# Score products of a pair's two heads, issued alternately into two PSUM banks

## The chip, the cores and the metric

The kernel runs on one core of one Trainium2 chip. The metric is the device time of one execution in microseconds (us); lower is better. The engines are named as in the profile: PE is the matrix engine (PEld its weight loads), DVE the vector engine, ACT the scalar engine, POOL GpSimd, SP the engine that issues the transfers.

## The reference

One decoder layer on 512 tokens of 1024 features, in fp32: a half-step of a gated feed-forward network, a token mixer, a second such half-step, and a gated embedding. The mixer is attention in a sliding window, with sinks, beside a causal convolution. Cut to what the change touches:

```python
q = partial_rope(rmsnorm(zq.reshape(B, S, 16, 64), q_norm), cos, sin)
k = partial_rope(rmsnorm(zk.reshape(B, S, 2, 64), k_norm), cos, sin)
# in sliding_window_attention: blocks of 128 queries, each with its own and the previous 128 keys
s = einsum('bnqhgd,bnkhd->bnhgqk', qb, kb) * scale
s = where(valid, s, -1e30)
m = maximum(max(s, axis=-1), sink)
pr = exp(s - m)
denom = sum(pr, axis=-1) + exp(sink - m)
o = einsum('bnhgqk,bnkhd->bnqhgd', pr / denom, vb)
...
u = causal_depthwise_conv(ca * sigmoid(cb), dw_w, dw_b)        # 31 taps
merged = sigmoid(ga) * (o @ attn_proj) + sigmoid(gb) * (silu(layernorm(u)) @ conv_proj)
x = x + merged @ w_out
```

There are 16 query heads of 64 features and 2 key heads, so 8 query heads share a key head.

## The kernel before

**Products.** Every fp32 operand is split into two parts, hi and lo. A product is three matmuls into one PSUM bank (`mm3`, lines 112 to 115): lo by hi (line 113), hi by hi (114), hi by lo (115). The hi part is made by ACT (line 88), the lo part by DVE (line 89; by POOL for the gates' weights). Parts are named by their endings _h and _l, those of weights whi and wlo.

**PSUM.** The eight banks are two pools of four: `pf` for projections (gates, convolution inputs, queries), `ps` for all else, the scores among it.

**Attention.** The heads stand in eight pairs: pair j holds query head j, whose features and key lie on the lower 64 partitions, and head j + 8, on the upper 64. A group g (0 or 1) is four pairs, a block t (0 to 3) 128 queries, so there are eight blocks (g, t). `scores` (lines 409 to 442) transposes a block's queries (qTp, split to qT), then makes eight score products of 64 partitions by 128 queries and 256 keys (128 keys at t = 0), which is 24 matmuls. Two products share a bank. In before the loop runs over the half hh, the half's two banks jj, and a bank's two pairs jl: all of a half before the other. After each product one DVE operation (line 438) masks and scales it to SBUF (s) and takes its row maximum (m). Four banks hold two rounds of what the trace calls sc. `softmax` (from line 444) takes the exponentials on ACT (454), the denominators on DVE (455, 456), and scales on POOL and ACT; `values` transposes the probabilities (pT, line 472), splits them (p_h, p_l) and multiplies them by the values into one bank (o), which ACT copies out (oF, line 484).

**Beside it** run the convolution's 31 taps for eight tiles of channels: on DVE (line 325) for five of them; for tiles 0, 2 and 4 ACT multiplies (ct, line 322) and POOL adds (323). Further the projections of the convolution's inputs (ca, cb), the queries (q_b), the gates (ga, gb), and attention's output (ap). sga and sgb are gates read out of PSUM by DVE.

**The order.** The string ORDER lists the mixer's parts in the order in which the program hands them over, and the convolution has a lower priority. The framework's scheduler then puts each engine's instructions into an order by its own simulated times, so that parts interleave, and an edit in one place moves instructions of all engines.

Of the kernel before, what the change touches and what calls it, by code (L numbers as in the profile page):

```python
# [15 lines left out]
P = 128  # L16
S = 512
NT = S // P
# [6 lines left out]
HD = 64  # L25
# [6 lines left out]
EPS = 1e-6  # L32
PIECE = 1024


# The order in which the mixer's parts are issued: K keys and values, Q a half of the queries;
# A scores, E softmax, V values of one block; a, b the convolution's input and its gate;
# g, h the gates' projections; p attention's projection; L the convolution's norm.
ORDER = """
# [7 lines left out]
def hybrid_layer(ctx: ExitStack, tc: tile.TileContext, a: dict, out: bass.AP):  # L47
    nc = tc.nc
# [35 lines left out]

# [1 line left out]
    def split_into(hi, lo, src, scale=None, eng=nc.vector):  # L86
# [14 lines left out]
    def piece(src, eng=nc.vector):  # L101
        """A weight piece [P, n] from DRAM as its two parts."""
        n = src.shape[1]
        raw = wraw.tile([P, PIECE], F32, tag="raw", name="raw")
        hi = wspl.tile([P, PIECE], F32R, tag="hi", name="whi")
        lo = wspl.tile([P, PIECE], F32R, tag="lo", name="wlo")
        nc.sync.dma_start(raw[:, 0:n], src)
        split_into(hi[:, 0:n], lo[:, 0:n], raw[:, 0:n], eng=eng)
        return hi, lo

    def mm3(ps, w, x, start, stop):
        """ps += w.T @ x of operands in two parts."""
        nc.tensor.matmul(ps, w[1], x[0], start=start, stop=False)  # L113
        nc.tensor.matmul(ps, w[0], x[0], start=False, stop=False)  # L114
        nc.tensor.matmul(ps, w[0], x[1], start=False, stop=stop)  # L115
# [3 lines left out]

# [1 line left out]
    def rsqrt(name, v, n):  # L121
        """1/sqrt(v) of a small positive tile by Newton's iteration."""
        y = small.tile([P, n], F32, tag=f"y{n}", name=f"{name}_y", bufs=2 if n > 8 else 4)
# [15 lines left out]
    def colsum(name, acc):  # L139
        """Sums over the partitions of [P, S], tokens on partitions: [P, NT] in PSUM."""  # L140
        ps = ps_tile(f"{name}_cs")
        for t in range(NT):
            nc.tensor.matmul(
                ps[:, t : t + 1], acc[:, t * P : (t + 1) * P], ones[:, 0:1], start=True, stop=True
            )
        return ps[:, 0:NT]
# [7 lines left out]
    def spread(name, r):  # L154
        """[P, NT], tokens on partitions, to [P, S] with tokens on the free axis, on each partition."""
        dg = tmp.tile([P, NT, P], F32, tag="t", name=f"{name}_dg")
# [27 lines left out]

# [1 line left out]
    g_all = const.tile([P, 8, KD], F32, name="g_all")  # L186
# [23 lines left out]
    def consts():  # L210
# [19 lines left out]

        # the gains of q's and k's unrotated parts are both k's
        qcs, kcs = table("qcs", gq), table("kcs", gk)
# [3 lines left out]
    def ffn(tag, wgu, wdown, h, ss, first, after):  # L236
        """x += 0.5 * swiglu; `after` takes each new tile of x."""
        rb = None
# [45 lines left out]

# [1 line left out]
    def proj(tag, w_piece, h, nk=KD, off=0, bank=None):  # L286
        """One [P, S] tile of h @ w, features on partitions."""
        ps = (bank or pf_tile)(tag)
# [20 lines left out]

    # depthwise causal convolution; some channels' taps are ScalarE's and GpSimd's  # L310
    def conv(c):
# [14 lines left out]

    # q, k, v with tokens on partitions
    def heads_rsqrt(tag, zs, n, scale):
        """scale / sqrt(mean of squares + EPS) of each head of each block of tokens."""
        v = small.tile([P, NT * n], F32, tag=f"hv{n}", name=f"{tag}_v", bufs=2)  # L330
# [9 lines left out]
    def rope(tag, z3, n, tab, t):  # L340
        """Gain and rotation of the rotated part of each head, in place."""
        w = tmp.tile([P, n, 16], F32, tag="rope", name=f"{tag}_w", bufs=2)
# [7 lines left out]
    def token_major(tag, pieces, kper, n):  # L350
        """h2.T @ w for each block of tokens: NT tiles in PSUM, several to a bank when they are small."""
        per = S // n
# [14 lines left out]
    kT = [rtile(f"kT{i}") for i in range(2)]  # L367
    # each part of v as [v0, 0, v1], so that a pair's heads take their own half of a column
    vp = [act.tile([P, 2, 3, HD], F32R, tag="a", name=f"v{t}", bufs=NBIG) for t in range(NT)]
# [25 lines left out]
    def queries(g):  # L395
        """Four pairs of heads (j, j + 8) of the queries, rotated; their norm and the scores' scale are in rq."""
        pss = token_major(f"q{g}_", [a["wq"][4 * g + i] for i in range(4)], 2, S)
# [11 lines left out]
    def scores(g, t):  # L409
        """Masked scores of eight heads (four pairs) of one block of queries, and their maxima."""  # L410
        pt = ps_tile(f"qTp{g}_{t}")
# [14 lines left out]
        mask = masks[:, min(t, 1), 0:nk]  # L426
        for hh in range(2):
            rows = slice(hh * HD, (hh + 1) * HD)
            for jj in range(2):
                ps = ps_tile(f"sc{g}_{t}_{hh}_{jj}").rearrange("p (j k) -> p j k", j=2)  # L430
                i0 = hh * 2 + jj
                for jl in range(2):
                    j = 2 * jj + jl
                    q = [qT[i][rows, j * P : (j + 1) * P] for i in range(2)]
                    kk = [kT[i][rows, k0 : k0 + nk] for i in range(2)]
                    mm3(ps[:, jl, 0:nk], q, kk, True, True)
                    i = 2 * i0 + jl
                    nc.vector.tensor_tensor_reduce(
                        s[i0][:, jl, 0:nk], ps[:, jl, 0:nk], mask, rq[g][t][:, 2 * j + hh : 2 * j + hh + 1],
                        sk[:, i : i + 1], ALU.add, ALU.max, m[:, i : i + 1],  # L440
                    )
# [63 lines left out]
    def attn_proj(o):  # L505
        """Attention's projection under its gate."""
        if o == 0:
# [15 lines left out]
    def conv_norm():  # L523
        """Layer norm over channels, then silu."""
        acc = tmp.tile([P, S], F32, tag="acc", name="ln_acc", bufs=2)
# [48 lines left out]

# [1 line left out]
    h4, ss4, after4 = next_norm("pg", g_gate)  # L576
# [11 lines left out]

# [1 line left out]
    rb4 = None  # L590
# [31 lines left out]
def _layout(inputs):  # L622
    """The inputs as the program reads them, and tables that depend on shapes alone."""
    import numpy as np
# [6 lines left out]
    def kxn(w):  # L631
        """[K, N] -> [N/128 tiles][128 of K, K/128, 128 of N]."""
        kt, nt = w.shape[0] // P, w.shape[1] // P
# [32 lines left out]

    rows = lambda v: np.broadcast_to(v, (P, v.shape[-1]))  # noqa: E731
    gains = np.stack(
# [53 lines left out]
```

## Time and profile before

| | us |
|---|---|
| median of 3 runs | 1309.3 |
| lowest, highest | 1308.62, 1310.32 |
| span of the profiled execution | 1306.9 |
| PE busy in it | 1241.3 |
| DVE busy | 804.9 |
| ACT busy | 496.8 |
| POOL busy | 379.5 |

The span is the time from the first to the last instruction of one profiled execution; the median lies 2.4 us above it. Numbers of the trace are told against the span's start. In a row of the timeline stand the start, the duration, the engine, the line, the operation, out<-in, the shapes and how many instructions the row joins, and in brackets how long the engine had been idle and what it waited for. In a row of waits stand who waited, for whom, the total in us, the times and the longest. In a row of stretches each engine's busy time is followed by its count of instructions in brackets, and at the end stand PE's granted clock (1.00 is full speed), the share of the DMA engines and GB/s.

### The profile page before, as it was taken

To read this page: it belongs to the slowest core of one execution; us is meant where nothing else is said; L and a number is where in the kernel's file an instruction comes from. 1 tells how busy PE (TensorE), PEld (TensorE's weight loads), DVE (VectorE), ACT (ScalarE), POOL (GpSimd) and SP (SyncE) were. 2 spreads that over 40 slices of the span, in tenths; PEclk is the share of its full clock that TensorE was granted. 3 is DMA by queue.
4 is the path that set the end of the run, shared out by engine and by line. 5 is a ranking of instruction groups with operands and counts; after the bars stand their busy time and mean duration, and the time that the engine had idled before them with its cause. 6 is when DMAs were issued, how large, how long until landed. Compare 5 with 4: busy or idle time off the path is not lost.

```text
span 1306.9 us, 14445 instructions
## 1 busy us (share of the span) xinstructions
PE 1241.3 (95%) x5534; PEld 1015.0 (78%) x5534; DVE 804.9 (62%) x1076; ACT 496.8 (38%) x789; POOL 379.5 (29%) x322
## 2 busy tenths in 40 slices
PE   7999999999999878786889999999999999999998
PEld 5888888888888666565767878888888888888886
DVE  7544444434448988999999665575444444444447
ACT  5333333222225457563755454333333333222242
POOL 4000000011116979867687350050000000011140
PEclk9999999999999989898988999999999999999999
DMA  6223222333322212121011123232232223333331
GB/s 210 97 97 97 97 97 97 89 100 94 101 95 71 80 49 65 49 65 49 17 49 65 65 97 113 81 113 83 97 99 98 95 97 98 96 89 105 109 97 65
DMA packets 35206, 115.27 MB, mean 88 GB/s; under 512 B 4416, under 2 KB 5952, under 8 KB 35136
## 3 DMA queue, kind: packets, MB, share of 16 engines
q1 hardware_dynamic: 34992, 114.31, 27.2%
q8 instruction: 43, 0.70, 0.2%
q14 instruction: 27, 0.22, 0.1%
q10 hardware_dynamic: 144, 0.03, 0.0%
HBM read 112.23 MB, written 2.10 MB: 87 GB/s over the span
## 4 chain that ended last, share of the span: by engine, by line
PE 75%; DVE 18%; ACT 3%; POOL 2%; issue 2%; DMA 0%; SPq 0%; DVEq 0%; POOLq 0%
DVE y L325 10%; PE f_d L114 6%; PE f_d L113 6%; PE f_d L115 6%; PE f_g L115 6%; PE f_u L115 6%; PE f_g L114 6%; PE f_g L113 6%; PE f_u L114 6%; PE f_u L113 6%; DVE wlo L89 2%; POOL y L323 1%; ACT s L454 1%; PE cp L113 1%; PE wo L115 1%
## 5 line engine op out<-in xcount | busy, mean ns | idle before, releaser
L88 ACT ACTIVATE whi<-raw 128x1024 fp32r<-128x1024 f32 (+1 forms) x210 | 219.4, 1045 | 566.9 <-PE f_u L115 258.6
L89 DVE TENSOR_TENSOR wlo<-raw,whi 128x1024 fp32r<-128x1024 f32 (+1 forms) x194 | 258.1, 1331 | 240.6 <-ACT whi L88 240.5
L325 DVE SCALAR_TENSOR_TENSOR y<-u,c_dww,y 128x511 f32<-128x511 f32 (+15 forms) x150 | 171.7, 1156 | 1.4
L323 POOL TENSOR_TENSOR y<-y,ct 128x511 f32<-128x511 f32 (+14 forms) x90 | 127.3, 1415 | 35.0 <-ACT ct L322 29.5
L113 PE MATMUL f_d<-f_a_h,wlo 128*128 128x512 f32 x352 | 137.1, 390 | 0.0
L115 PE MATMUL f_d<-f_a_l,whi 128*128 128x512 f32 x352 | 137.1, 389 | 0.0
L114 PE MATMUL f_d<-f_a_h,whi 128*128 128x512 f32 x352 | 137.1, 389 | 0.0
L257 DVE TENSOR_TENSOR f_gs<-f_g,f_n_rb 128x512 f32<-128x512 f32 x44 | 30.4, 691 | 104.7 <-PE f_g L115 95.9
L322 ACT ACTIVATE ct<-u,c_dww 128x511 f32<-128x511 f32 (+14 forms) x90 | 62.4, 707 | 65.7 <-POOL y L323 65.2
L113 PEld LDWEIGHTS f_d<-f_a_h,wlo 128*128 128x128 f32 x352 | 66.1, 188 | 13.8
L115 PEld LDWEIGHTS f_d<-f_a_l,whi 128*128 128x128 f32 x352 | 66.1, 188 | 13.7
L114 PEld LDWEIGHTS f_d<-f_a_h,whi 128*128 128x128 f32 x352 | 66.1, 188 | 13.6
L180 POOL TENSOR_TENSOR pg_ss_acc<-xt 128x512 f32<-128x512 f32 x1 | 1.0, 1040 | 252.9 <-DVE xt L270 252.9
L180 POOL TENSOR_TENSOR mix_ss_acc<-xt 128x512 f32<-128x512 f32 x1 | 1.0, 1039 | 235.2 <-DVE xt L270 235.2
L113 PE MATMUL f_u<-f_h_h,wlo 128*128 128x512 f32 x176 | 69.0, 392 | 0.0
L113 PE MATMUL f_g<-f_h_h,wlo 128*128 128x512 f32 x176 | 68.7, 390 | 0.0
L115 PE MATMUL f_u<-f_h_l,whi 128*128 128x512 f32 x176 | 68.6, 390 | 0.0
L114 PE MATMUL f_g<-f_h_h,whi 128*128 128x512 f32 x176 | 68.6, 390 | 0.0
L114 PE MATMUL f_u<-f_h_h,whi 128*128 128x512 f32 x176 | 68.6, 390 | 0.0
L115 PE MATMUL f_g<-f_h_l,whi 128*128 128x512 f32 x176 | 68.6, 390 | 0.0
L113 PE MATMUL f_u<-h_h,wlo 128*128 128x512 f32 x168 | 65.9, 392 | 0.0
L115 PE MATMUL f_u<-h_l,whi 128*128 128x512 f32 x168 | 65.5, 390 | 0.0
(320 smaller groups left out, 2883.7 us busy)
## 6 DMA issues: line engine op xcount, KB each, us to landing
raw<-in_wgu SPq DMA_DIRECT2D x86, 512.0 KB, 3.5
raw<-in_wd SPq DMA_DIRECT2D x32, 512.0 KB, 3.6
raw<-in_wzc SPq DMA_DIRECT2D x16, 512.0 KB, 3.5
raw<-in_wzg SPq DMA_DIRECT2D x16, 512.0 KB, 3.4
raw<-in_wd SPq DMA_DIRECT2D x16, 384.0 KB, 3.1
raw<-in_wq SPq DMA_DIRECT2D x8, 512.0 KB, 3.4
raw<-in_wap SPq DMA_DIRECT2D x8, 512.0 KB, 3.5
raw<-in_wcp SPq DMA_DIRECT2D x8, 512.0 KB, 3.4
```

Source lines behind the costliest of these rows:

```text
L88: nc.scalar.activation(hi, src, AF.Copy)
L89: eng.tensor_tensor(lo, src, hi.bitcast(F32), op=ALU.subtract)
L113: nc.tensor.matmul(ps, w[1], x[0], start=start, stop=False)
L114: nc.tensor.matmul(ps, w[0], x[0], start=False, stop=False)
L115: nc.tensor.matmul(ps, w[0], x[1], start=False, stop=stop)
L180: nc.gpsimd.tensor_tensor(to, v, v, op=ALU.mult)
L257: nc.vector.tensor_tensor(g, pg, rb, op=ALU.mult)
L322: nc.scalar.activation(t, ud, AF.Copy, scale=wk)
L323: nc.gpsimd.tensor_tensor(yd, yd, t, op=ALU.add)
L325: nc.vector.scalar_tensor_tensor(yd, ud, wk, yd, op0=ALU.mult, op1=ALU.add)
L454: nc.scalar.activation(si, si, AF.Exp, bias=nm[:, i : i + 1], accum_out=den[:, i : i + 1])
```

## The change

`scores` takes two banks at a time, one for each half hh, and issues the three matmuls of the two halves' products alternately; the two DVE readings follow the six matmuls. The diff also takes comments and docstrings out, and all lines below move by ten (the reading is line 448 instead of 438).

```diff
-        for hh in range(2):
-            rows = slice(hh * HD, (hh + 1) * HD)
-            for jj in range(2):
-                ps = ps_tile(f"sc{g}_{t}_{hh}_{jj}").rearrange("p (j k) -> p j k", j=2)
-                i0 = hh * 2 + jj
-                for jl in range(2):
-                    j = 2 * jj + jl
-                    q = [qT[i][rows, j * P : (j + 1) * P] for i in range(2)]
-                    kk = [kT[i][rows, k0 : k0 + nk] for i in range(2)]
-                    mm3(ps[:, jl, 0:nk], q, kk, True, True)
+        for jj in range(2):
+            pss = [
+                ps_tile(f"sc{g}_{t}_{hh}_{jj}").rearrange("p (j k) -> p j k", j=2) for hh in range(2)
+            ]
+            for jl in range(2):
+                j = 2 * jj + jl
+                for n, (a_, b_) in enumerate(((1, 0), (0, 0), (0, 1))):
+                    for hh in range(2):
+                        rows = slice(hh * HD, (hh + 1) * HD)
+                        nc.tensor.matmul(
+                            pss[hh][:, jl, 0:nk],
+                            qT[a_][rows, j * P : (j + 1) * P],
+                            kT[b_][rows, k0 : k0 + nk],
+                            start=n == 0,
+                            stop=n == 2,
+                        )
+                for hh in range(2):
+                    i0 = hh * 2 + jj
                     i = 2 * i0 + jl
                     nc.vector.tensor_tensor_reduce(
-                        s[i0][:, jl, 0:nk], ps[:, jl, 0:nk], mask, rq[g][t][:, 2 * j + hh : 2 * j + hh + 1],
+                        s[i0][:, jl, 0:nk], pss[hh][:, jl, 0:nk], mask, rq[g][t][:, 2 * j + hh : 2 * j + hh + 1],
```

The instructions stay the same in kind and number. Their order changes on PE, DVE, ACT and POOL from the first score product on; SP's stays. Three places follow; the digits behind sc are t, hh and jj and the bank's running number, those behind p and pT are t, hh, the block of keys and the running number.

PE, first round of the block g = 0, t = 0, before and then now:

```order
L113 MATMUL sc_0_0_0_3258<-kT_2548,qT_0_l 128x128
L114 MATMUL sc_0_0_0_3258<-kT_2548,qT_0_h 128x128
L115 MATMUL sc_0_0_0_3258<-kT_2549,qT_0_h 128x128
L113 MATMUL sc_0_0_1_3267<-kT_2548,qT_0_l 128x128
L114 MATMUL sc_0_0_1_3267<-kT_2548,qT_0_h 128x128
L115 MATMUL sc_0_0_1_3267<-kT_2549,qT_0_h 128x128
L113 MATMUL sc_0_1_0_3276<-kT_2548,qT_0_l 128x128
```

Now the same block begins so on PE:

```order
L438 MATMUL sc_0_0_0_3258<-kT_2548,qT_0_l 128x128
L438 MATMUL sc_0_1_0_3259<-kT_2548,qT_0_l 128x128
L438 MATMUL sc_0_0_0_3258<-kT_2548,qT_0_h 128x128
L438 MATMUL sc_0_1_0_3259<-kT_2548,qT_0_h 128x128
L438 MATMUL sc_0_0_0_3258<-kT_2549,qT_0_h 128x128
L438 MATMUL sc_0_1_0_3259<-kT_2549,qT_0_h 128x128
L438 MATMUL sc_0_0_1_3276<-kT_2548,qT_0_l 128x128
```

The halves alternate within the first round, and a bank's third product comes fifth instead of third. In the second round, which begins when DVE has read the banks, the scheduler puts two matmuls of one bank side by side in places:

```order
L438 MATMUL sc_0_0_0_3258<-kT_2548,qT_0_l 128x128
L438 MATMUL sc_0_0_0_3258<-kT_2548,qT_0_h 128x128
L438 MATMUL sc_0_1_0_3259<-kT_2548,qT_0_l 128x128
L438 MATMUL sc_0_1_0_3259<-kT_2548,qT_0_h 128x128
L438 MATMUL sc_0_0_0_3258<-kT_2549,qT_0_h 128x128
L438 MATMUL sc_0_1_0_3259<-kT_2549,qT_0_h 128x128
```

There the pairs of one bank's first two matmuls stand together, and only the last two alternate.

ACT, block g = 1, t = 1 (p_3 are the splits of the probabilities of group 0's last block, es and s the exponentials of this one, ct the products of a tap), before:

```order
L88 ACTIVATE p_3_0_1_h<-pT_3_0_1_4521 128x512
L88 ACTIVATE p_3_1_0_h<-pT_3_1_0_4530 128x512
L88 ACTIVATE p_3_1_1_h<-pT_3_1_1_4539 128x512
L448 ACT_TABLE_LOAD
L448 ACTIVATE es_1_4596<-es_1_4596 128x8
L454 ACTIVATE s_1_0_4469,den_1_4601<-s_1_0_4469,nm_1_4599 128x256 x2
L454 ACTIVATE s_1_1_4470,den_1_4601<-s_1_1_4470,nm_1_4599 128x256 x2
L454 ACTIVATE s_1_2_4471,den_1_4601<-s_1_2_4471,nm_1_4599 128x256 x2
L454 ACTIVATE s_1_3_4472,den_1_4601<-s_1_3_4472,nm_1_4599 128x256 x2
L322 ACTIVATE ct_6_4108<-u_4089,c_dww 128x506
```

The same place on ACT now:

```order
L88 ACTIVATE p_3_0_1_h<-pT_3_0_1_4521 128x512
L322 ACTIVATE ct_6_4108<-u_4089,c_dww 128x506
L88 ACTIVATE p_3_1_0_h<-pT_3_1_0_4530 128x512
L458 ACT_TABLE_LOAD
L458 ACTIVATE es_1_4596<-es_1_4596 128x8
L464 ACTIVATE s_1_0_4469,den_1_4601<-s_1_0_4469,nm_1_4599 128x256 x2
L464 ACTIVATE s_1_1_4470,den_1_4601<-s_1_1_4470,nm_1_4599 128x256 x2
L464 ACTIVATE s_1_2_4471,den_1_4601<-s_1_2_4471,nm_1_4599 128x256 x2
L88 ACTIVATE p_3_1_1_h<-pT_3_1_1_4539 128x512
L464 ACTIVATE s_1_3_4472,den_1_4601<-s_1_3_4472,nm_1_4599 128x256 x2
```

The split p_3_1_1_h moved from ahead of the table load to behind six exponentials, and the tap ct_6 from behind them to ahead of it. On DVE p_3_1_1_l stands in both orders ahead of the convolution input u and the denominators den_1; now one tap more (482 columns) stands ahead of these splits.

DVE, the last block's splits of the probabilities (g = 1, t = 3; y_4838 is the convolution's last tile, and the second number of its shape tells the tap), before:

```order
L89 TENSOR_TENSOR p_3_0_0_l<-pT_3_0_0_5382,p_3_0_0_h 128x512
L325 SCALAR_TENSOR_TENSOR y_4838<-u_4836,c_dww,y_4838 128x488
L89 TENSOR_TENSOR p_3_0_1_l<-pT_3_0_1_5391,p_3_0_1_h 128x512
L325 SCALAR_TENSOR_TENSOR y_4838<-u_4836,c_dww,y_4838 128x487
L89 TENSOR_TENSOR p_3_1_0_l<-pT_3_1_0_5400,p_3_1_0_h 128x512
L325 SCALAR_TENSOR_TENSOR y_4838<-u_4836,c_dww,y_4838 128x486
L325 SCALAR_TENSOR_TENSOR y_4838<-u_4836,c_dww,y_4838 128x485
L325 SCALAR_TENSOR_TENSOR y_4838<-u_4836,c_dww,y_4838 128x484
L325 SCALAR_TENSOR_TENSOR y_4838<-u_4836,c_dww,y_4838 128x483
```

The same place on DVE now:

```order
L325 SCALAR_TENSOR_TENSOR y_4838<-u_4836,c_dww,y_4838 128x487
L89 TENSOR_TENSOR p_3_0_0_l<-pT_3_0_0_5382,p_3_0_0_h 128x512
L89 TENSOR_TENSOR p_3_0_1_l<-pT_3_0_1_5391,p_3_0_1_h 128x512
L325 SCALAR_TENSOR_TENSOR y_4838<-u_4836,c_dww,y_4838 128x486
L325 SCALAR_TENSOR_TENSOR y_4838<-u_4836,c_dww,y_4838 128x485
L325 SCALAR_TENSOR_TENSOR y_4838<-u_4836,c_dww,y_4838 128x484
L89 TENSOR_TENSOR p_3_1_0_l<-pT_3_1_0_5400,p_3_1_0_h 128x512
L325 SCALAR_TENSOR_TENSOR y_4838<-u_4836,c_dww,y_4838 128x483
```

The taps of 486, 485 and 484 columns moved from behind p_3_1_0_l to ahead of it. The split p_2_1_1_l, some ten places earlier, has the taps of 489 and 488 ahead of it that stood behind it, and on PE three products of a gate (ga) moved ahead of the matmul that takes it.

Smaller moves of the same kind: on DVE a tap (503 columns, tile 3) now stands ahead of the first reduction q_v of group 1's query norm, which takes a result of POOL (q_sq); on ACT one tap's product (ct 26 of tile 0) stands ahead of the first table load, and in the block g = 0, t = 1 both p_h of block 0 stand ahead of the exponentials, with one tap's product between them, where one of them stood among them.

## The prediction

> **What bounds the kernel now.** I read the page first: the busy times, the 40 slices and the chain that ended last. Then the busy times of stretches, the waits of PE and of DVE, and at last single rows of the timeline.
>
> ```profile
> span 1306.9 us, 14445 instructions
> PE 1241.3 (95%) x5534; PEld 1015.0 (78%) x5534; DVE 804.9 (62%) x1076; ACT 496.8 (38%) x789; POOL 379.5 (29%) x322
> DVE  7544444434448988999999665575444444444447
> PE 75%; DVE 18%; ACT 3%; POOL 2%; issue 2%; DMA 0%; SPq 0%; DVEq 0%; POOLq 0%
> ```
>
> PE is busy for 95% of the span, which invites the conclusion that any PE time saved is time won. The DVE slices say otherwise for one part: slices 13 to 22 (a slice is 32.7 us) read 8 or 9, and the chain that ended last lies on DVE for 18% of the span. That part is the token mixer, and it holds all the score products. The busy times there, with three smaller stretches and the whole rest of the program:
>
> ```profile
> 440.00:720.00 280.00, 233.60 (x1059) 183.44 (x1058) 265.93 (x416) 160.84 (x355) 220.38 (x190) 0.90 0.16 52
> 610.00:620.00 10.00, 6.49 (x27) 5.59 (x28) 10.00 (x25) 1.54 (x3) 5.04 (x3) 0.50 0.17 53
> 720.00:1300.00 580.00, 578.49 (x2559) 477.10 (x2558) 307.74 (x375) 189.56 (x240) 86.83 (x50) 1.00 0.29 95
> 510.00:520.00 10.00, 10.00 (x55) 8.20 (x54) 8.96 (x15) 5.80 (x9) 9.92 (x12) 1.00 0.33 105
> 550.00:570.00 20.00, 20.00 (x91) 15.56 (x89) 18.86 (x40) 13.87 (x31) 10.53 (x13) 0.91 0.22 67
> ```
>
> The columns after the length are PE, weight loads, DVE, ACT and POOL, then PE's granted clock. From 440 to 720 us DVE is busy for 265.93 of 280 (95%), PE for 233.60 (83%); from 720 on PE is busy for 578.49 of 580. So the mixer goes at DVE's pace, and the rest at PE's. What PE waits for in the mixer, and after it:
>
> ```profile
> PE sc L113 <- DVE m L438: 17.8, 6, 8.2
> PE sc L113 <- DVE qT_l L89: 9.1, 2, 7.5
> PE pT L472 <- DVE m L438: 5.0, 5, 1.8
> PE o L115 <- DVE p_l L89: 4.3, 3, 3.1
> ```
>
> ```profile
> PE ap L113 <- DVE wlo L89: 1.3, 1, 1.3
> PE o L115 <- DVE p_l L89: 0.7, 1, 0.7
> ```
>
> The first four alone are 36.2 us, all for DVE, and the largest is a score product that waits until DVE has read its bank. In the second list (712 us to the end) almost nothing is left: the 1.3 us stand behind DVE's work on the convolution's norm, which itself is released by PE and so moves with it. Hence the **end** is the moment at which DVE releases PE for the last time in the mixer, plus a tail of PE work that the change leaves alone. That moment is this row, a product of the last block's values, 0.72 us late for DVE's split of the probabilities:
>
> ```profile
> 711.68 0.50 PE L115 MATMUL o<-p_l,v 128*128 128x512 f32 x1 [0.72 <-DVE p_l L89]
> 698.26 5.31 DVE L325 SCALAR_TENSOR_TENSOR y<-u,c_dww,y 128x492 f32<-128x492 f32 x3
> 711.55 2.98 DVE L325 SCALAR_TENSOR_TENSOR y<-u,c_dww,y 128x486 f32<-128x486 f32 x4
> ```
>
> The two rows of DVE give the price of a convolution tap, on which much below rests: 5.31 / 3 = 1.77 us while POOL adds beside it, 2.98 / 4 = 0.745 us while POOL doesn't.
>
> **The change part by part. The products themselves.** There are 192 matmuls of 64 partitions, three to a score product; they start this far apart:
>
> ```profile
> 485.77 0.28 PE L114 MATMUL sc<-kT,qT_h 64*128 64x256 f32 x1
> 485.89 0.28 PE L115 MATMUL sc<-kT,qT_h 64*128 64x256 f32 x1
> ...
> 474.01 0.27 PE L113 MATMUL sc<-kT,qT_l 64*128 64x128 f32 x1
> 474.12 0.27 PE L114 MATMUL sc<-kT,qT_h 64*128 64x128 f32 x1
> ```
>
> The step is 0.12 us with 256 columns and 0.11 with 128, so it isn't the moving columns that set it: 192 x 0.115 = 22 us. If alternate halves ran fully side by side, half of it, 11 us, would go from PE's busy time; if not at all, nothing. No row of before shows two halves alternating, so both ends stand. For the span I take 0 of it, because DVE reads each product more slowly than PE makes it:
>
> ```profile
> 485.50 0.55 DVE L438 CUSTOM_DVE_ANT_0 s<-sc,c_masks,sk 128x256 f32<-128x256 f32 x1 [0.71 <-PE sc L115]
> 485.97 0.54 DVE L438 CUSTOM_DVE_ANT_0 s<-sc,c_masks,sk 128x256 f32<-128x256 f32 x1
> ```
>
> DVE takes 0.47 us per product, PE 3 x 0.115 = 0.35 already. In the trace DVE waits for a score product once, 0.7 us:
>
> ```profile
> DVE den L455 <- ACT s L454: 6.1, 4, 3.3
> DVE p_l L89 <- ACT p_h L88: 3.1, 2, 2.3
> DVE q_v L334 <- POOL q_sq L333: 1.0, 1, 1.0
> DVE s L438 <- PE sc L115: 0.7, 1, 0.7
> ```
>
> There the alternate order puts two products of the other bank ahead of the awaited third: +0.23 us without overlap, 0 with it. I take +0.1.
>
> The Trainium skill, "TensorEngine Tiling (Array Packing)", Key Properties, says that different tiles of the array load weights and multiply in parallel, and its Gotcha 1 that different row tiles need different PSUM banks, which is what the change arranges. By that rule PE would get the whole 11 us; the trace of before cannot show it, and with DVE at 95% the page's own remark on the PSUM Bottleneck (evacuation becomes the limit once TensorE is faster) agrees with the 0.47 against 0.35 us.
>
> **What the scheduler moved.** All engines' orders change in the mixer, though the instructions are the same; SP's queue of transfers keeps its order. Three moves touch a wait of DVE or the last release.
>
> First, the block of group 0, t = 0 and 1. In before ACT reached the first p_h only behind taps that waited for POOL, and DVE waited 2.3 us for it:
>
> ```profile
> 491.00 0.72 ACT L322 ACTIVATE ct<-u,c_dww 128x510 f32<-128x510 f32 x1 [0.40 <-POOL y L323]
> 491.62 0.58 ACT L88 ACTIVATE p_h<-pT 128x512 fp32r<-128x512 f32 x1
> 496.12 0.49 ACT L454 ACTIVATE s<-s,nm 128x256 f32<-128x256 f32 x1
> ```
>
> Now one tap (ct 26) goes ahead of the first exponentials, so POOL is a tap ahead, and both p_h stand ahead of the exponentials. ACT's last exponential should end 0.5 us earlier (496.1 for 496.6), at most a tap's 1.1 us, at least nothing: -0.5. One more gain: a DVE tap now stands ahead of the reduction q_v that waited 1.0 us for POOL: -1.0 (between -1.0 and 0).
>
> Second, group 1, t = 1:
>
> ```profile
> 620.51 0.60 ACT L88 ACTIVATE p_h<-pT 128x512 fp32r<-128x512 f32 x1 [0.26 <-PE pT L472]
> 621.12 1.28 ACT L448 ACT_TABLE_LOAD   x1
> 622.53 0.49 ACT L454 ACTIVATE s<-s,nm 128x256 f32<-128x256 f32 x1
> 621.06 1.28 DVE L89 TENSOR_TENSOR p_l<-pT,p_h 128x512 fp32r<-128x512 f32 x2
> 626.60 0.17 DVE L455 TENSOR_TENSOR den<-den,es 128x8 f32<-128x8 f32 x1 [1.80 <-ACT s L454]
> ```
>
> The fourth p_h ran at 620.51, ahead of the table load. Now it stands behind the load and six of the eight exponentials: 622.53 + 6 x 0.49 + 0.60 = 626.1, and only then can DVE split it. DVE's split before that one, the first of the two at 621.06, ended at 621.7; one tap more (482 columns) stands ahead of it now, so DVE is free at about 622.3 and waits 3.8 us, where it waited 1.8 at the denominators: +2.0, or 0 if PE's transposes come so late that DVE waits for them either way. At the same place a tap of ACT (ct 6) goes ahead of the table load, and POOL adds it while DVE waits instead of beside one of DVE's taps later: between 0 and 1.77 - 0.745 = 1.0 us saved; I take -0.7, nearer the latter, as POOL is busy beside DVE for 79% of the mixer.
>
> Third, the last release. p_3_1_0_l stood behind the tap of 487 columns; now it stands behind those of 486, 485 and 484 as well. At 0.745 each: **+2.2 us**. Two taps more (489 and 488) stand ahead of p_2_1_1_l too, the release before that, with three gate products of PE (0.7 us) moved ahead to cover it: beside POOL 2 x 1.77 - 0.7 = 2.8, less the 0.72 us that PE waited at the last release, 2.1, so both ways give about the same. The bounds are 0 (if DVE arrives at the whole place earlier by as much) and three taps beside POOL, +5.3.
>
> DVE's lateness in between is not made up, as its window of 610 to 620 us shows no slack; POOL's and ACT's other moves of one place I take as nothing, since DVE waits for them in no row.
>
> **The sum.** +0.1 - 0.5 - 1.0 + 2.0 - 0.7 + 2.2 = +2.1 us. The profiled span of 1306.9 becomes 1309.0; the median of the runs, 1309.3, is 2.4 above that span, so **1311.4**. The lower bounds add to 0 - 1.1 - 1.0 + 0 - 1.0 + 0 = -3.1, the upper ones to 0.23 + 0 + 0 + 2.0 + 0 + 5.3 = +7.5: 1306.2 to 1316.8, the latter only if every term is at its worst. A measurement of this kernel can tell 0.2%, about 2.6 us, from no change.
>
> **The rivals.** *PE leads after all.* In 510 to 520 and 550 to 570 us PE was busy for 100% and DVE for 90 and 94%. The score products in these stretches:
>
> ```profile
> 510.00:520.00 10.00, 0.97 (x6) 0.77 (x6) 1.99 (x4) 1.00 0.33 105
> 550.00:570.00 20.00, 2.80 (x21) 2.01 (x19) 4.04 (x9) 0.91 0.22 67
> ```
>
> Half of 3.77 is 1.9 us less, and then what the scheduler moved to DVE's loss would be hidden as well (without +2.0 and +2.2): 1311.4 - 1.9 - 4.2 = 1305.3, faster. Against it: what PE gains there is waited away at its next stop for DVE. By the skill's rule taken at its full size, with PE the bound everywhere, it would be 1309.3 - 11 = 1298.3. Chance 0.10.
>
> *A stall that cools PE.* The scheduler mostly keeps the second round (the banks' second use) bank by bank, and a second-round product that stands at PE's head before DVE has read the bank holds up all that is behind it:
>
> ```profile
> 612.88 0.58 PE L113 MATMUL sc<-kT,qT_l 64*128 64x256 f32 x1 [8.24 <-DVE m L438]
> ```
>
> After this stall PE's clock was 0.50 for 610 to 620 us, with 6.49 us of work in it. At full clock that work takes 3.2 us less. One more stall of this length, in a place where PE's lateness reaches DVE (the transposes pT, then p_h, p_l), costs those 3.2: 1311.4 + 3.2 = 1314.6, slower. It decides as soon as PE is later with pT than DVE with its queue of taps. For it: there are six waits of this kind already; against it: DVE nearly always has a tap to do. Chance 0.18.
>
> *The change does not do what it says.* The step stays 0.115 us because each product's weight load sets it, whichever half it uses; only the moves act: +2.1 with the full 0.23 for 0.1, so 1311.5. The Trainium skill, "TensorE: Matmul & The Clock Gate", Part 3, has weight loads overlap running products only when the row groups differ, which speaks for an overlap here; but in before the loads of one half already keep a step of 0.115 us. Chance 0.12.
>
> **How the numbers follow.** The main case has 0.60: 0.07 faster, 0.32 the same, 0.21 slower, as its value lies just inside the line of 0.2% (1311.9). The first rival adds 0.08 to faster and 0.02 to the same, the second 0.18 to slower, the third 0.08, 0.02 and 0.02 to same, slower and faster. Together 0.17, 0.42 and 0.41. The range takes in the main case's bounds and the second rival with some of its spread, and the first rival's nearer value: 1305.0 to 1316.5.
>
> **What would show it.** If right: score steps of 0.06 to 0.115 us between the alternate halves; PE's busy time from 440 to 720 us lower by up to 11 us with DVE's about the same; PE's waits for DVE in the mixer longer by what PE saved; DVE's wait for p_3_1_1_h in group 1, t = 1, near 3.8 us; the last o product of p_3_1_0_l some 2 us later than 711.68 (by the program's own time); and everything behind it shifted alike. Wrong would be: a mixer whose DVE busy time itself falls or grows by several us (then POOL's additions have moved against DVE's taps by more than one tap), or a PE that is late for DVE in several blocks.

## The result, and the profile after

| | before | after |
|---|---|---|
| median of 4 runs, us | 1309.4 | 1318.1 |
| lowest, highest | 1308.62, 1310.32 | 1317.13, 1318.32 |
| span of the profiled execution | 1306.9 | 1316.3 |
| DVE busy in it | 804.9 | 808.1 |
| PE busy in it | 1241.3 | 1239.0 |

The kernel became slower: the ratio of the times is 1.0066, with a 95% interval of 1.0054 to 1.0078. The time lies 1.6 us above the range that was predicted. First the page of the changed kernel: span, busy times, DVE's slices, the chain that ended last.

```profile
span 1316.3 us, 14455 instructions
...
PE 1239.0 (94%) x5534; PEld 1010.8 (77%) x5534; DVE 808.1 (61%) x1076; ACT 497.1 (38%) x789; POOL 376.5 (29%) x322
...
DVE  7544444444448979999999566575444444444447
...
PE 74%; DVE 19%; ACT 3%; issue 2%; POOL 1%; DMA 0%; SPq 0%; DVEq 0%; POOLq 0%; ACTq 0%
```

PE works 2.3 us less and the span is 9.4 us longer, so the loss isn't PE's work. DVE works 3.2 us more, though its instructions are the same. The stretch of the mixer, and the worst 20 us of it, in after (columns as in the prediction: PE, weight loads, DVE, ACT, POOL, PE's clock):

```profile
440.00:720.00 280.00, 222.48 (x1017) 172.50 (x1016) 262.65 (x405) 156.21 (x345) 217.73 (x187) 0.88 0.15 51
600.00:620.00 20.00, 5.39 (x28) 4.58 (x29) 19.75 (x25) 2.38 (x3) 14.28 (x8) 0.55 0.18 63
```

In the same 280 us fewer instructions get done: 405 of DVE for 416 before, 1017 of PE for 1059. In the 20 us DVE is busy for 19.75 and PE for 5.39. Then the waits of PE and of DVE from 440 to 740 us (total, times, longest):

```profile
PE sc L438 <- DVE qT_l L89: 19.5, 5, 9.8
PE sc L438 <- DVE m L448: 8.4, 5, 5.0
PE pT L482 <- DVE m L448: 8.0, 5, 2.4
PE o L115 <- DVE p_l L89: 7.9, 7, 3.9
```

```profile
DVE den L465 <- ACT s L464: 7.4, 3, 5.3
DVE p_l L89 <- ACT p_h L88: 6.3, 3, 4.3
...
DVE s L448 <- PE sc L438: 0.7, 1, 0.7
```

PE still waits for DVE, and more of it falls on the split of the queries (qT_l). DVE waits for ACT, at two places for longer than before; its one wait for a score product is 0.7 us in both kernels.

**Where the 9.4 us lie.** They are complete at the last release. Before, the product of p_3_1_0_l started at 711.68 and the span ended 595.2 us later. Now:

```profile
721.15 0.50 PE L115 MATMUL o<-p_l,v 128*128 128x512 f32 x1 [0.64 <-DVE p_l L89]
```

721.15 + 595.2 = 1316.3, the span. So the whole loss stands ahead of this row, on DVE's way to that split. PE is nearly as late by itself: it waits 0.64 us here, and waited 0.72 in before. Each DVE instruction of before was matched with the same one of after, from the first qT_l (at 463 us) to the start of p_3_1_0_l. The lateness of a row then splits into three parts: longer waits, instructions that stand ahead of it now and didn't before (less the opposite), and the same instructions taking longer.

```
DVE row (time before)                     late   waits   order   same instructions slower
qT_1_l of g=1,t=1        (600.55)         8.25    0.42    8.86   -0.78
first p_l in g=1,t=1     (619.08)         2.10    0.42    1.27    0.66
qT_2_l of g=1,t=2        (628.87)         3.10    3.12   -1.40    1.64
first p_0 in g=1,t=2     (637.57)         7.85    3.12    1.97    3.01
p_2_1_0_l in g=1,t=3     (697.66)         7.16    3.12    0.00    4.29
p_3_1_0_l                (710.96)         9.46    3.12    2.15    4.44
```

The three parts of the last row add to 9.7; the first split began 0.25 us earlier. Until 600 us after isn't late at all: the 8.25 us at qT_1_l are mostly taps that stand ahead of it now, five more than before, and by the next row all but 2.1 us of it has come back.

*Waits, +3.1.* The first is the largest at the start: the denominators of the block g = 0, t = 0. In after (ACT's rows, then DVE's):

```profile
476.50 1.28 ACT L322 ACTIVATE ct<-u,c_dww 128x488 f32<-128x488 f32 x2
479.89 0.71 ACT L322 ACTIVATE ct<-u,c_dww 128x486 f32<-128x486 f32 x1 [2.10 <-POOL y L323]
480.61 1.28 ACT L458 ACT_TABLE_LOAD   x1
...
485.24 0.17 DVE L465 TENSOR_TENSOR den<-den,es 128x8 f32<-128x8 f32 x1 [5.28 <-ACT s L464]
```

And in before:

```profile
476.98 1.28 ACT L448 ACT_TABLE_LOAD   x1
...
482.43 0.17 DVE L455 TENSOR_TENSOR den<-den,es 128x8 f32<-128x8 f32 x1 [3.28 <-ACT s L454]
```

The tap of 486 columns (ct 26), now at ACT's head, waits 2.10 us for POOL to free its buffer, and the table load with all the exponentials stands behind it: DVE waits 5.28 us for 3.28. The other changes in this block and the next (2.28 to 1.79, 0.87 to 0, 0.29 to 0.93) bring the sum there to +1.3. The q_v reduction's wait of 1.04 is gone. The third large one is p_3_1_1_l in g = 1, t = 1:

```profile
620.28 0.60 ACT L88 ACTIVATE p_h<-pT 128x512 fp32r<-128x512 f32 x1 [11.19 <-PE pT L482]
...
627.20 0.57 ACT L88 ACTIVATE p_h<-pT 128x512 fp32r<-128x512 f32 x1
...
627.81 0.69 DVE L89 TENSOR_TENSOR p_l<-pT,p_h 128x512 fp32r<-128x512 f32 x1 [4.26 <-ACT p_h L88]
```

Its p_h runs at 627.20, behind the load and six exponentials. With 0.24 at the split before it, DVE waits 4.5 us where it waited 1.8.

*Order, +2.15.* The three taps of 486 to 484 columns ahead of the last split took 2.23 us as a row: 718.27 in the next fence.

*The same instructions slower, +4.4.* The taps of the last tile (y_4838) take 4.1 us more and those of the tile ahead of it (y_4688) 1.2; all else together 0.8 less. By the table 4.29 of it are there at 697 us, ahead of the tail, but the tail's rows show best what a tap costs. DVE and POOL in after:

```profile
705.42 8.70 DVE L325 SCALAR_TENSOR_TENSOR y<-u,c_dww,y 128x492 f32<-128x492 f32 x5
714.64 1.27 DVE L501 TENSOR_TENSOR sga<-ga,mix_n_rb 128x512 f32<-128x512 f32 x2
...
718.27 2.23 DVE L325 SCALAR_TENSOR_TENSOR y<-u,c_dww,y 128x486 f32<-128x486 f32 x3
...
705.87 3.27 POOL L540 TENSOR_TENSOR ln_acc<-ln_acc,y 128x512 f32<-128x512 f32 x2
709.11 2.80 POOL L89 TENSOR_TENSOR wlo<-raw,whi 128x1024 fp32r<-128x1024 f32 x1
711.87 1.72 POOL L540 TENSOR_TENSOR ln_acc<-ln_acc,y 128x512 f32<-128x512 f32 x1
```

And in before:

```profile
704.09 1.27 DVE L491 TENSOR_TENSOR sga<-ga,mix_n_rb 128x512 f32<-128x512 f32 x2
...
705.88 1.79 DVE L325 SCALAR_TENSOR_TENSOR y<-u,c_dww,y 128x489 f32<-128x489 f32 x1
...
708.20 1.15 DVE L325 SCALAR_TENSOR_TENSOR y<-u,c_dww,y 128x488 f32<-128x488 f32 x1
...
703.00 2.77 POOL L323 TENSOR_TENSOR y<-y,ct 128x483 f32<-128x483 f32 x2
705.84 4.66 POOL L530 TENSOR_TENSOR ln_acc<-ln_acc,y 128x512 f32<-128x512 f32 x3
```

A tap beside POOL takes 8.70 / 5 = 1.74 us on average (0.90 for the first, half over when POOL begins, 2.73 for the one beside POOL's split of weights, 1.64 for the others), and 2.23 / 3 = 0.74 when POOL is idle. The gate readings sga, which read PSUM, take 0.64 us each beside POOL's addition (704.09 in before) as well as with POOL idle (714.64 in after). In before DVE did such readings while POOL worked; in after five taps stand there. Summed over DVE's taps from 569 us to the last split (each from its start to that of the next instruction, without waits), the time that lay beside POOL's work went from 79.6 to 86.5 us; for the readings of PSUM (scores, gates, splits) it fell from 25.0 to 20.4. The group of the taps shows the sum on the page, in before and in after:

```profile
L325 DVE SCALAR_TENSOR_TENSOR y<-u,c_dww,y 128x511 f32<-128x511 f32 (+15 forms) x150 | 171.7, 1156 | 1.4
```

```profile
L325 DVE SCALAR_TENSOR_TENSOR y<-u,c_dww,y 128x511 f32<-128x511 f32 (+19 forms) x150 | 174.9, 1178 | 1.7
```

The same 150 taps take 3.2 us more, which is DVE's whole rise in busy time.

### The profile page after: what moved, and what is told of

Read it like the earlier page. It is cut to its first block, busy times and chain, and to the rows that moved or that the text cites. A ratio compares the mean times of both kernels' runs of the same rounds, so it can differ in the third digit from the quotient of the medians.

```text
span 1316.3 us, 14455 instructions
## 1 busy us (share of the span) xinstructions
PE 1239.0 (94%) x5534; PEld 1010.8 (77%) x5534; DVE 808.1 (61%) x1076; ACT 497.1 (38%) x789; POOL 376.5 (29%) x322
## 4 chain that ended last, share of the span: by engine, by line
PE 74%; DVE 19%; ACT 3%; issue 2%; POOL 1%; DMA 0%; SPq 0%; DVEq 0%; POOLq 0%; ACTq 0%
DVE y L325 10%; PE f_d L115 6%; PE f_d L114 6%; PE f_d L113 6%; PE f_g L113 6%; PE f_g L115 6%; PE f_u L113 6%; PE f_u L115 6%; PE f_u L114 6%; PE f_g L114 6%; DVE wlo L89 2%; ACT s L464 2%; DVE s L448 1%; PE wo L113 1%; PE cp L113 1%
## 5 line engine op out<-in xcount | busy, mean ns | idle before, releaser
L325 DVE SCALAR_TENSOR_TENSOR y<-u,c_dww,y 128x511 f32<-128x511 f32 (+19 forms) x150 | 174.9, 1178 | 1.7
```

The costliest lines, as they stand in the source:

```text
L325: nc.vector.scalar_tensor_tensor(yd, ud, wk, yd, op0=ALU.mult, op1=ALU.add)
```

## The experiments

The theory after the result: the loss is the order, by the three parts above, and the alternating products themselves cost nothing. The rivals: the products themselves delay DVE or PE; or a single place makes the loss and the rest is hidden behind it.

To part order and products, the kernels below take the changed program and chain the mixer's instructions on PE, DVE, ACT and POOL in a listed order, by links that affect the issue order alone and add no wait between engines. ISSUE holds 1042 instructions of PE, 332 of DVE, 285 of ACT and 174 of POOL; in the last four runs, which shorten POOL's work, it holds the whole program:

```diff
+def keep_order(nc, tc):
+    made = {i.name: i for i in nc.cur_bb.bb.instructions}
+    link = mybir.DependencyInfo(mybir.DependencyClass.NoSync, mybir.DependencyReason.DATA)
+    for listed in ISSUE.values():
+        names = []
+        for part in listed.split():
+            a, _, b = part.partition("-")
+            names += [f"I-{n}" for n in range(int(a), int(b or a) + 1)]
+        for a, b in zip(names, names[1:]):
+            tc.add_manual_dep(made[b], a, link, reason="order")
...
         hybrid_layer(tc, aps, out)
+        keep_order(nc, tc)
```

In the diffs below, which show rows of the order that results, "-" is the kernel named ahead and "+" the experiment. All results first; the ratio is to before in the same runs, the last four columns are DVE's lateness at p_3_1_0_l against before and its parts as above (they leave out at most 0.7 us that stood ahead of the first split). Span and parts are read from one profiled execution, and executions of one kernel differ: those of alt_order_before went from 1308.6 to 1313.1 us, and the profiled one is the fastest of them. The parts aren't quite independent either: while DVE waits, POOL goes on, and less of its work stands beside the taps afterwards (1.0 us more of waits and 0.7 less of the last part in the first row).

| run | median (runs) | ratio, interval | span | late | waits | order | slower |
|---|---|---|---|---|---|---|---|
| alt_order_before | 1311.0 (11) | 1.0010, 1.0001 to 1.0019 | 1306.8 | -0.1 | 1.0 | 0 | -0.7 |
| plain_order_after | 1318.3 (5) | 1.0064, 1.0052 to 1.0077 | 1317.2 | 10.4 | 3.1 | 2.1 | 4.6 |
| after_then_before | 1314.7 (5) | 1.0039, 1.0027 to 1.0052 | 1314.2 | 4.3 | 4.8 | 0 | -0.3 |
| after_first_half | 1307.9 (11) | 0.9989, 0.9981 to 0.9998 | 1306.1 | -0.7 | 0 | 0 | -0.8 |
| mix_best | 1307.5 (12) | 0.9985, 0.9976 to 0.9994 | 1305.7 | -1.2 | -0.3 | 0 | -0.7 |
| after_repair_g1t1 | 1314.7 (5) | 1.0047, 1.0034 to 1.0060 | 1311.9 | 5.1 | 1.2 | 2.1 | 1.0 |
| only_g1t1 | 1315.2 (4) | 1.0050, 1.0035 to 1.0065 | 1314.3 | 7.4 | 5.3 | 0 | 2.7 |
| only_mid | 1313.8 (5) | 1.0037, 1.0023 to 1.0052 | 1311.6 | 1.8 | 3.1 | 0 | -1.4 |

**Alternate products in before's order.** PE, against before (one first round):

```diff
 sc_1_0_0 <- qT_1_l
-sc_1_0_0 <- qT_1_h
-sc_1_0_0 <- qT_1_h
-sc_1_0_1 <- qT_1_l
+sc_1_1_0 <- qT_1_l
+sc_1_0_0 <- qT_1_h
+sc_1_1_0 <- qT_1_h
```

> The changed kernel's products, alternating between the halves, with every other instruction of PE, DVE, ACT and POOL in before's order (the alternate products fill the places that the score products had). Theory A (the loss is the order that the scheduler chose, not the alternation): 1309.4 us, within 1.0 of before. Theory B (the alternate matmuls or the two banks cost time themselves): 1316 to 1318 us. Theory C (alternate halves overlap and PE's saving reaches the end): 1306 us or less. In the trace PE's pairs of score products start under 0.03 us apart if they overlap.

**Products head by head in after's order.** PE, against after:

```diff
 sc_1_0_0 <- qT_1_l
+sc_1_0_0 <- qT_1_h
+sc_1_0_0 <- qT_1_h
 sc_1_1_0 <- qT_1_l
-sc_1_0_0 <- qT_1_h
 sc_1_1_0 <- qT_1_h
-sc_1_0_0 <- qT_1_h
 sc_1_1_0 <- qT_1_h
```

> The counterpart: all engines in the changed kernel's order, but the three products of one half stand together again ahead of those of the other half, in the same places. Theory A: 1318 us, within 1.0 of the changed kernel. Theory B: 1309 to 1311 us. Theory C: more than 1319, as the overlap is lost.

The two separate the causes. With before's order the alternate products put the median 1.6 us above before's (0.1 to 2.5 by the interval), where 1.0 was expected at most; the profiled span of 1306.8 hides this, as the median of the eleven spans is 1309.2. With after's order and no alternation the loss of after is there in full, with all three parts of it. So **the order makes the loss**, 6 us or more of the 8.7; the alternation adds nothing that shows in after's order, and up to 2.5 us in before's. One row of waits of alt_order_before tells of a cost on DVE:

```profile
DVE s L448 <- PE sc L438: 1.9, 2, 1.2
```

DVE waits 1.9 us for score products, where it waits 0.7 in before and in after; the new wait, 1.18 us at 555.97, is the 1.0 of the table. What makes the median's 1.6 wasn't followed further.

What the products gained is smaller than thought. All 192 score products, PE, weight loads and DVE's readings, in the stretch of 440 to 720 us: of before, of after, of alt_order_before, and of plain_order_after.

```profile
440.00:720.00 280.00, 28.35 (x192) 22.95 (x192) 29.78 (x64) 0.90 0.16 52
```

```profile
440.00:720.00 280.00, 25.14 (x192) 19.77 (x192) 29.37 (x64) 0.88 0.15 51
```

```profile
440.00:720.00 280.00, 24.63 (x192) 17.20 (x192) 29.81 (x64) 0.89 0.15 51
```

```profile
440.00:720.00 280.00, 24.50 (x192) 19.49 (x192) 29.36 (x64) 0.90 0.15 51
```

PE saves 28.35 - 25.14 = 3.2 us, and head by head in after's order it saves as much. The reason stands in PE's rows of plain_order_after. Its program order is l, h, h of one half and then l, h, h of the other (l and h for products with the queries' lo and hi part):

```profile
488.66 0.39 PE L438 MATMUL sc<-kT,qT_l 64*128 64x256 f32 x2 [0.54 <-DVE qT_l L89]
488.88 0.40 PE L438 MATMUL sc<-kT,qT_h 64*128 64x256 f32 x4
```

The records show the two l first (0.01 us apart) and then the four h. They don't name the half, but by the program's order the second l is the other half's: as far as the records tell, PE started its products beside the first's by itself, out of program order. In before it did so too where a product of the other half came within reach:

```profile
485.18 0.28 PE L115 MATMUL sc<-kT,qT_h 64*128 64x256 f32 x1
485.19 0.39 PE L113 MATMUL sc<-kT,qT_l 64*128 64x256 f32 x2
485.42 0.28 PE L114 MATMUL sc<-kT,qT_h 64*128 64x256 f32 x2
```

Of 191 steps from one score product to the next, 28 are under 0.03 us in before, 63 in after, 58 in plain_order_after and 84 in alt_order_before.

**After's order, but before's from p_2_1_1_l on (from about 710 us of after's time).** DVE, against after:

```diff
-y_4838 128x489
-y_4838 128x488
 p_2_1_1_l
...
-y_4838 128x487
+y_4838 128x489
 p_3_0_0_l
+y_4838 128x488
 p_3_0_1_l
+y_4838 128x487
+p_3_1_0_l
 y_4838 128x486
...
-p_3_1_0_l
```

> Alternate products; the changed kernel's order on all engines up to the second last block's splits (DVE: four taps behind its third split p_2_1_0_l of group 1, about 710 us), then before's order. Only the last release is undone. Theory A with the tail at 2.15 us of the lag of 9.5 on DVE: 1318.1 - 2.2 = 1315.9 us. If the tail is all of the loss: 1309 us. If it is nothing, because PE is as late by other ways: 1318 us.

Against after the median falls by 3.4 us, the span by 2.1. The order of the tail is worth more than its three taps: with before's tail the last part of the table falls from 3.5 us at p_2_1_0_l to -0.3 at the last split. So DVE is 5.1 us earlier there than in after, but PE can't use it all: at this place PE no longer waits for DVE at all.

```profile
719.17 0.39 PE L115 MATMUL o<-p_l,v 128*128 128x512 f32 x1
```

This row, without a wait, is the product of p_3_1_0_l, whose split started at 715.30. 719.17 + 595.2 = 1314.4, the span within 0.2. PE itself is 7.5 us later than in before, from what it waited earlier in the mixer.

**After's order until 605 us, before's from there.** ACT, against after, where the orders change over:

```diff
 p_3_0_1_h
-ct_6
 p_3_1_0_h
+p_3_1_1_h
 ACT_TABLE_LOAD
```

> Alternate products; the changed kernel's order up to the block g = 1, t = 1 (about 605 us), then before's order to the end. DVE's row of the tap with 496 columns stood 0.7 us earlier in the changed kernel than in before, in spite of the 2.0 us more that DVE waited in the first block. Theory A: 1308.7 us (1308 to 1310). If the longer wait of the first block is what costs, and the earlier tap is chance: 1311.4 us.

**The same, and before's order until 490 us too,** so that after's order holds from 490 to 605 us alone. ACT, against after_first_half:

```diff
 ct_25
-ct_26
 ACT_TABLE_LOAD
...
+ct_26
 ct_27
```

> Alternate products; before's order in the first block (up to the last score reading of g = 0, t = 1, about 490 us, which takes the tap ct 26 back behind the first exponentials), the changed kernel's order from there to about 605 us, then before's order. Theory A (each piece of order carries its own gain or loss on DVE): the 2.0 us of longer wait in the first block go, less what the earlier tap brought (0.5 and 0.9): 1306.5 us, 1305 to 1308. If the pieces don't add: 1308 to 1309.

Until 605 us after's order costs nothing on balance, and between 490 and 605 us it gains. mix_best is faster than both kernels, by 0.15% (0.06 to 0.24%), and its last release sits where its time says it should:

```profile
710.50 0.50 PE L115 MATMUL o<-p_l,v 128*128 128x512 f32 x1 [0.72 <-DVE p_l L89]
```

710.50 + 595.2 = 1305.7, its span. Before's order until 490 us, with ct_26 behind the exponentials, is worth 0.5 us of DVE's lateness, not 2.0: the wait at the denominators is back at 3.28 us, but the next split then waits 2.92 us for its p_h instead of 1.78.

**After, but before's order in g = 1, t = 1 (605 to 635 us); and the opposite, before with after's order there alone.** ACT, the second against alt_order_before:

```diff
 p_3_0_1_h
+ct_6
 p_3_1_0_h
-p_3_1_1_h
 ACT_TABLE_LOAD
```

> The changed kernel in all but one block: from about 605 to 635 us (g = 1, t = 1, with the fourth p_h ahead of the table load again) all engines stand in before's order. Theory A1 (that block costs 4.8 us on DVE, 2.7 of them waits, and the later slower taps of 3 us are their own): 1313.3 us. Theory A2 (the later slower taps come from the lateness of that block): 1310 us. If only the wait counts: 1315.4 us. If the block is nothing: 1318 us.

> Alternate products; before's order, but from about 605 to 635 us (group 1, t = 1) the changed kernel's: the fourth p_h behind six exponentials, one tap more ahead of it, qT of t = 1 later. Theory A1 (that block carries a loss of its own of 4.8 us on DVE, 2.7 in waits and some 2 in slower taps): 1309.5 + 4.8 = 1314.3 us. If only the wait counts: 1312.2. If the block's loss needs what stands around it in the changed kernel: 1309.5.

**Before with after's order from 635 to 705 us alone.** POOL, against alt_order_before:

```diff
+y_4091 128x497
 s_2_0 x2
 s_2_1 x2
 s_2_2 x2
-wlo
-y_4091 128x497
+y_4091 128x496
 wlo
-y_4091 128x496
 y_4091 128x495
```

> Alternate products; before's order, but from about 635 to 705 us (group 1, t = 1 to 2, with the scores of t = 2 and 3) the changed kernel's, in which DVE never waits, so that all its loss would be slower taps. If these are a property of the order there: 1309.5 + 3 to 4 = 1313 us. If they come from the lateness of what stands ahead: 1309.5.

The block g = 1, t = 1 alone costs 6.3 us against before in the same runs, the stretch after it 5.0, and taking the block out of after gives 3.4 back, between the values that were expected if the block's whole loss or its wait alone went. The taps behind it stay slow without it: from the row at 619 us to the last split the last part of the table still grows by 4.1 us, for 3.8 in after. The pieces don't add: together they would be 11.3 with no tail, and after has lost 8.7 with it. In only_g1t1 the same wait as in after stands there:

```profile
628.62 0.69 DVE L89 TENSOR_TENSOR p_l<-pT,p_h 128x512 fp32r<-128x512 f32 x1 [4.26 <-ACT p_h L88]
```

Behind it come 1.3 us of further waits, which after's own order of the next block avoids; with 1.3 ahead of it for a score product, as in alt_order_before, the waits are the 5.3 of the table. In only_mid the time came out as expected, but not by slower taps alone: DVE waits 3.1 us more (1.2 of them ahead of that stretch), and the slower taps are 2.5 us at p_2_1_0_l and gone at the last split. DVE is 4.8 us late at p_2_1_0_l, and with before's tail only 1.8 at the last split, but PE is late itself by then, as in after_then_before. So no single place makes the loss.

**Is it POOL's work that slows the taps?** Two pairs, each with both orders kept as they were. The first shortens POOL's additions of tile 4:

```diff
-                nc.gpsimd.tensor_tensor(yd, yd, t, op=ALU.add)
+                n = 8 if c == 4 and d >= 6 else S - d
+                nc.gpsimd.tensor_tensor(yd[:, 0:n], yd[:, 0:n], t[:, 0:n], op=ALU.add)
```

> Before's order with alternate products, but POOL adds only 8 columns of the products of tile 4's taps 6 to 30 (the rest of these taps is left out of the output), so that POOL is hardly beside DVE between 620 and 705 us. DVE's work on the same instructions gets about 15 us shorter there; the counterpart is few_adds_after.

> The changed kernel's order with the same few columns in POOL's additions. If DVE's taps are longer in the changed kernel (4.4 us over the mixer) because they stand beside more of POOL's additions, the difference between this and few_adds_before in DVE's time for the same instructions, behind 620 us, is under 1.5 us, and the kernels differ by under 6 us; if DVE's longer taps have another cause, the 3 to 4 us behind 620 us stay.

The second shortens the sums of the convolution's norm and group 1's scaling of the probabilities as well:

```diff
+                si = si[:, 0:8] if g == 1 else si
...
-                nc.gpsimd.tensor_tensor(acc, acc, ys[c], op=ALU.add)
+                nc.gpsimd.tensor_tensor(acc[:, 0:8], acc[:, 0:8], ys[c][:, 0:8], op=ALU.add)
```

> As few_adds_before, and POOL's sums for the convolution's norm and its scaling of group 1's probabilities are cut to 8 columns as well (the rest is left out of the output), so that of POOL's work beside DVE behind 610 us the splits of weights alone stay. Under 1298 us.

> The changed kernel's order with the same cuts. Theory P (DVE's slower taps in the changed kernel come from standing beside POOL's scaling, norm sums and additions, with which they overlapped 3.2, 2.1 and 2.0 us longer, while the reads from PSUM overlapped that much less): against less_pool_before DVE's time for the same instructions behind 605 us differs by under 1 us, where it was 5 us in the full kernels and 4.4 with the few additions. If it stays at 3 us or more, POOL isn't the cause.

| pair (one run each) | before's order | after's order | difference | waits | order | slower |
|---|---|---|---|---|---|---|
| as it is (spans) | 1306.9 | 1316.3 | 9.4 | 3.1 | 2.15 | 4.4 |
| few_adds (spans) | 1297.8 | 1305.6 | 7.8 | 1.9 | 2.2 | 4.4 |
| less_pool (spans) | 1291.8 | 1296.4 | 4.6 | 3.1 | 2.2 | -1.5 |

Less work on POOL makes the kernel faster although POOL is busy for under a third of the span: with the additions cut, 9.1 us, and with the rest 15.1. The first pair went against its expectation: the third part stayed at 4.4 us, so those of the additions that it shortens alone don't make the difference between the orders. In that pair DVE's taps stood beside POOL's scalings for 3.9 us more in after's order, beside the sums for 2.2 and beside the additions for 1.9. With scalings and sums cut too, the third part is gone, and even turns to -1.5. The group of the taps on the pages of less_pool_before and less_pool_after:

```profile
L326 DVE SCALAR_TENSOR_TENSOR y<-u,c_dww,y 128x511 f32<-128x511 f32 (+15 forms) x150 | 156.9, 1057 | 1.4
```

```profile
L326 DVE SCALAR_TENSOR_TENSOR y<-u,c_dww,y 128x511 f32<-128x511 f32 (+19 forms) x150 | 154.5, 1042 | 1.7
```

The 150 taps take 14.8 us less than in before (171.7), and the order of after no longer makes them slower; their time beside POOL differs by 1.0 us between the two orders, where it differed by 6.9. So the slower taps come from POOL's work beside them, the scalings and sums being needed for the difference; which of these two counts for how much wasn't tried apart. The spans of these pairs tell it less well than the parts: each is a single run, and in all four kernels PE no longer waits for the last split, so the span isn't set by DVE's last release there.

## Why the prediction was wrong

It gave 0.41 to slower and named no change as likeliest, at +2.1 us; the span rose by 9.4, more than all its upper bounds together (+7.5).

- **The bound held.** DVE paces the mixer, and the end is its last release plus a fixed tail: 595.2 us in before, after, mix_best and only_g1t1 alike. It reaches only so far, though: in after_then_before, only_mid and the four kernels with less of POOL's work PE came later than that split, so a gain on DVE alone is soon cut off by PE's own lateness. The predicted sign that DVE's busy time would show it, if POOL's work had moved against the taps, is what came.
- **The products themselves: 0 of the span, right in after's order.** DVE's one wait for a score product stayed 0.71 us. (In before's order the alternation put 1.6 us on the median.) The working missed a row, though: "no row of before shows two halves alternating" was wrong, as PE already paired 28 steps in before by itself. So 3.2 us went from PE's busy time, near the lower end of the 0 to 11 that was given. The Trainium skill, "TensorE: Matmul & The Clock Gate", Part 3, says that weight loads overlap running products when the row groups differ, and the trace agrees: in plain_order_after a load starts at 488.664 us beside the product that runs from 488.656 for 0.38. It also has matmuls start strictly in program order, and there the records of plain_order_after (l, l, h, h, h, h) differ.
- **The first block: -0.5 predicted, +1.3 measured.** The step that failed is "one tap (ct 26) goes ahead of the first exponentials, so POOL is a tap ahead". ACT works in its order, and the tap had to wait 2.10 us for POOL; the bounds, -1.1 to 0, left this out.
- **q_v: -1.0, right** (1.04 to 0).
- **Group 1, t = 1: +2.0 predicted, +2.7 measured.** The mechanism was the one named. It was sized 0.7 us too small, as p_3_1_1_h ended at 627.8, not at 626.1, while DVE was free at 623.55 instead of 622.3: the first p_h of the block, released by PE's transposes, came at 620.28 where it had come at 617.71, behind PE's wait of 9.8 us for qT_l and at a clock of 0.55. That is like the second rival's mechanism, at a fifth of its price; how much of it is the clock wasn't tried apart.
- **The last release: +2.2, right** (2.15). The two taps ahead of p_2_1_1_l were beside POOL, as it was said.
- **POOL beside DVE: -0.7 predicted, +4.4 measured.** This is the miss that decides, 5.1 of the 7.4 us. The step was that "POOL's and ACT's other moves of one place I take as nothing, since DVE waits for them in no row". They cost DVE no wait but its speed: a tap is 1.0 us longer beside POOL, and a reading of PSUM isn't. The prediction looked at one tap's addition, and not at which kind of DVE's work the rest of POOL's came to stand beside. The Trainium skill, "SBUF — State Buffer", Who interferes with whom, has this distinction: a DVE instruction with two inputs in SBUF collides with a GpSimd instruction that reads SBUF, one with at most one such input doesn't, outside the modes that use both ports. The rows agree with it (1.74 and 0.74 us for a tap; 0.64 for sga beside POOL and apart from it).

The terms add up: 5.1 + 1.8 + 0.7, with the small rest of -0.2 (other waits +0.2, the third product -0.1, the start -0.25, the tail -0.05), are the 7.4 us between +2.1 and the 9.46 of lateness. *PE leads after all* fell: PE's 3.2 us are not in the span. *The change does not do what it says* held in part, since PE pairs two halves that stand close by, however their products are listed.

## What to carry to other kernels

Where a scheduler lays out the whole program, compare a local edit first in the old order: an order kept by links that add no wait tells in a few runs whether the edit or its echo moves the time. Before a saving on an engine is counted, look whether it is the one that paces the stage; here a part of the score products' gain was there already (28 of 191 steps for 63) and the rest was waited away. And when the pacing engine's instructions are moved, count what stands beside them as well as what stands ahead: DVE's operations on two SBUF inputs belong beside an idle POOL, its readings of PSUM beside a busy one.

## What the hardware showed that was not expected

- By the records, PE starts matmuls of the other 64 rows ahead of earlier ones of its own queue: with a program order of l, h, h, l, h, h the starts came in pairs 0.01 us apart, l with l and h with h. In before's first round, with six products of one half ahead, the other half's first started 0.35 us after the first of all, beside the third, as far as the pairs tell.
- POOL, busy for 29% of the span, costs some 15 us of it beside DVE's taps: shortening its additions, sums and scalings took 14.8 us from the taps and 15.1 from the span (less_pool_before, one run). DVE's rows of waits don't show it: its only wait for POOL in the mixer is 1.0 us (q_v), and that stays.
